# A hybrid decoder trunk on one core: where the norm's blocks turn between two layers, and in which order they come back

## The chip, the core and the metric

The kernel runs on one core of a Trainium2 chip. The metric is device time in microseconds; a run is one execution of the whole program. Five engines work side by side, each through its own list of instructions in order: TensorE (PE, with its weight loads as PEld), VectorE (DVE), ScalarE (ACT), GpSimd (POOL) and SyncE (SP). POOL and SP here mainly issue DMAs, each on a queue of its own: POOL's is the software queue q0, SP's the hardware queue q1.

## The reference

A trunk of two layers over 256 tokens of width 2048, in float32. Layer 0 mixes with gated linear attention, layer 1 with forgetting attention, whose keys and values come from the residual stream after layer 0. Every layer also attends to 256 memory tokens, and ends in a gated channel mixer. What stands around the change is this:

```python
def fox_shared_kv(x, g_kv, w_kv, b_f):
    hs = rmsnorm(x, g_kv)
    k, v, fl = split_cols(hs @ w_kv, [FOX_WIDTH, FOX_WIDTH, FOX_HEADS])
    ...

def rmsnorm(x, g):
    xf = x.astype(jnp.float32)
    y = xf * lax.rsqrt(jnp.mean(xf * xf, axis=-1, keepdims=True) + EPS)
    return (y * g.astype(jnp.float32)).astype(x.dtype)
```

`x` is the residual stream after layer 0's channel mixer, whose last step is a down-projection of hidden width 5632 to 2048, added to `x`. `FOX_WIDTH` is 1536: twelve heads of 128.

## The kernel before, in words

**Arithmetic.** Each float32 product is made of three TensorE products: data and weights are both split into a high and a low part, and high by high, high by low and low by high are added. Weights come from device memory in units of 512 KB (`split_unit`: load on SP's queue, L224, into one of four buffers `raw`; the high part is copied on ScalarE, L229; the low part subtracted on VectorE, L230). A unit's buffer is free for the next load once both are done. TensorE's matmuls of a panel of 512 output columns are at L333 (`panel_tm`): for 128 x 512 output there is a pair of token halves and a chain over chunks of 128 input features.

**The residual and its blocks.** `x[f]`, f = 0 to 3, holds 512 columns each, tokens on the partitions. The next layer needs features on the partitions. So each block f, once its two token halves are added (`add_to`, L483), goes through `then(f, b)` in `preparing`: the halves' squares are summed on ScalarE (`StreamNorm.add`, L608), each half is transposed in squares of 32 on VectorE (L1586) into a buffer `blk`, and, after the second half, `far_away` (L629 to L640) writes the block to device memory (L632) on POOL's queue. `land()` takes the oldest block that is away and issues its four returns (L637), which bring it back with the squares rearranged. `take()` takes the oldest block that landed and splits it, with the norm's gain, into four chunks of `hk`, whose buffers the profile calls B (ScalarE L524, VectorE L526). Block f gives chunks 4f to 4f+3. The buffer `blk` exists twice, so that block 2's transposes need block 0's way out to have landed, and block 3's need block 1's. Blocks 0 to 2 land in three parts of the tile `fvt`, block 3 in a tile called `fky`.

**The order at the seam.** The first layer's channel mixer, `ffn(0)`, ends with a pair of down panels (`down_pair`, blocks 0 and 1, evacuated through `late`) and two single ones, `f2` and `f3`, for blocks 2 and 3, each of six units. The hooks are written out by hand:

```python
for u in (4, 5):
    f2(u)
    then.land()
for u in range(2, 6):
    f3(u)
    if u % 2:
        then.take()
```

Then `fox` begins with its key panels, `two_tm([fk(0), fk(1)], 8, 2, hooks)`: two panels of eight units of two chunks each, interleaved, the second starting behind, with hooks at chosen units: the other returns and takes, and the row of the norm (`nx.row`, two matmuls at L593). A scheduler orders the built program by priorities and by what each step needs, so that the order in the source is a wish, and the built order can differ from it.

**The parked memory.** The first layer's hidden values need more chunks than there are buffers. So two tiles of projected memory, `mk1` and `mv1`, are stored to device memory before `ffn(0)`, their places carry four chunks more (`moremk`, `moremv` in the profile), and `fox` reloads them, 512 KB each, on POOL's queue (L1141 to L1143). They are needed only where layer 1 attends to the memory.

Of the kernel before, what the change touches and what calls it, by code (L numbers as in the profile page):

```python
# [20 lines left out]
P = 128  # L21
# [124 lines left out]
def _trunk(ctx: ExitStack, tc: tile.TileContext, xt, xtok, memt, wp, wgu, gns, gfin, cnv, par, msk, out):  # L146
# [984 lines left out]
    def fox(nx, vt, stash):  # L1131
        hk, hq, mix = bufB, bufA, bufB
        with (
# [4 lines left out]
            cdram = dp.tile([FOX_H, T], F32, name="cdram")  # L1138
            kt = fp.tile([P, FOX_H, T], F32, name="fkt")

            for t, tag, far in ((mk, "mk1", parked[0]), (mv, "mv1", parked[1])):  # L1141
                t[1] = const.tile(list(t[1].shape), F32, name=tag + "again", tag=tag)
                nc.gpsimd.dma_start(t[1].rearrange("p a b -> p (a b)"), far)  # L1143
            spare = [const.tile([P, 4, 4, 2, 32], F32, name="fky", tag=t) for t in ("mk0", "mv0")]
            last = blocks_of(kt[:, 8:].rearrange("p h t -> p (h t)"))
            open_ = []
# [1 line left out]
            def fk(j):  # L1148
                y, z = (spare[0], spare[1]) if j == 0 else (last, spare[0 if j == 1 else 1])

                return panel_tm(("fk", j), hk, turn_out(y, lambda back: open_.append((j, back, z))), j == 1)
# [9 lines left out]
            def query_input(i):  # L1161
                split_turned(hq, i, (*stash, spare[1])[i // 4], "mix1")

            two_tm([fk(0), fk(1)], 8, 2, {(0, 2): nx.land, (0, 3): nx.take, (1, 2): nx.row,
                                          (1, 3): lambda: nx.land(spare[1]), (1, 5): nx.take})
            step = fk(2)
            for u in range(8):
# [22 lines left out]
            for j, (lo, hi) in enumerate(FV_PARTS):  # L1190
                def fv_out(b, a, j=j, lo=lo, hi=hi):
                    S.activation(vt[:, b, lo:hi], a[:, : hi - lo], AF.Copy, scale=nx.col()[:, b : b + 1])
                    if j == 0:
                        take(b, a[:, hi - lo :])
                        if b:
                            forget()

                step = panel_tm(("fv", j), hk, fv_out)
                for u in range(8):
                    step(u)  # L1200
                    if (j, u) in ((0, 0), (0, 2), (1, 2)):
                        keys()
                    if j == 0:
                        query_input(4 + u)

# [106 lines left out]
    def down_pair(l, p, f, src, sums, flip, pool, temps, then=None):  # L1312

        def early(bank):
            t0, t1 = temps()
            S.activation(t0, bank["p1"], AF.Copy)
            add_to(f)(0, t0)
            V.tensor_tensor(t0, bank["p6"], t0, ALU.add)
            V.tensor_tensor(t1, bank["p7"], t0, ALU.add)
            add_to(f)(1, t1)  # L1320
            add_to(f + 1)(1, t1)
            add_to(f + 1)(1, bank["p5"])
            V.tensor_tensor(t0, bank["p5"], t0, ALU.add)
            add_to(f + 1)(0, t0)

        def late(b, h, a):
            add_to(f + h)(b, a)
            if then is not None:
                then(f + h, b)

        return pair_steps(where["down", l, p, f], src, sums, flip, pool, early, late)
# [26 lines left out]
    def ffn(l, nx, h, m, ys, zs, landing, then, pool, temps, last=None, spare=None):  # L1358
        with tc.tile_pool(name=f"ffn{l}", bufs=1) as fp:
# [159 lines left out]
            if l:  # L1519
                f2, f3 = [rows_tm(("down", l, p, f), src, evac) for f, evac in ((2, third), (3, last))]  # L1520
            else:
                f2 = panel_tm(("down", l, p, 2), src, third)
                f3 = panel_tm(("down", l, p, 3), src, lambda b, a: (add_to(3)(b, a), then(3, b)))
            for k in range(8):
# [14 lines left out]
            if l:  # L1539
                for u in (4, 5):  # L1540
                    f2(u)
                for b in range(2):
                    for u in range(2 if b else 4, 6):
                        f3(u, (b,))
            else:
                for u in (4, 5):
                    f2(u)
                    then.land()
                for u in range(2, 6):
                    f3(u)  # L1550
                    if u % 2:
                        then.take()

    def preparing(name, dst, pool, far, kept=None, tag="blk", queue=nc.sync):

        n = StreamNorm()  # L1560
        blocks = {}
        away, landed = [], []

        def land(z=None):

            f, back = away.pop(0)
            if z is None:
                z = pool.tile([P, 4, 4, 2, 32], F32, name="turn", tag="turn", bufs=2) if kept is None else kept[f]
            with tc.issue_after(loads[-1].ins) if queue is nc.sync else nullcontext():
                back(flat(z))  # L1570
            landed.append((f, z))

        def take():

            f, z = landed.pop(0)
            with tc.issue_after(casts[-1].ins):
                for k in range(4):
                    split_turned(dst, 4 * f + k, z, name)

        def then(f, b):  # L1580
            n.add(f, b)
            with tc.high_priority(offset=AHEAD):
                if b == 0:
                    blocks[f] = pool.tile([P, 4, 4, 2, 32], F32, name="blk", tag=tag, bufs=2)
                y = blocks[f]
                V.transpose(y[:, :, :, b, :], x[f][:, b, :].rearrange("p (k c i) -> p c k i", c=4, i=32))  # L1586
                if b:
                    away.append((f, far_away(far, flat(y), T, queue)))

        n.land = then.land = land  # L1590
        n.take = then.take = take
        return n, then
# [31 lines left out]
    with tc.tile_pool(name="store", bufs=1) as op:  # L1624
        gf = []
        free = list(range(8))

        def spare():
            return place("A", free.pop(0), "spare").rearrange("p a t -> p (a t)")

        def begin():
            for f in range(4):
                gf.append(place("A", 12 + f, "gf", F32).rearrange("p a t -> p (a t)"))
                nc.sync.dma_start(gf[f], gfin[:, f * 512 : (f + 1) * 512].to_broadcast([P, 512]))

        def temps(i):
            return op.tile([P, 512], F32, name="temp", tag=f"temp{i}")

        junk = op.tile([P, 1], F32, name="junk")

        def then(f, b):
            fin.add(f, b)
            if f == 0 and b == 0:
                S.activation(junk, fin.sums[:, 0, 0:1], AF.Sqrt)
            V.tensor_tensor(x[f][:, b, :], x[f][:, b, :], gf[f], ALU.mult)

        def last(b, a):

            part = sm.tile([P, 1], F32, name="fp", tag="fp")
            V.tensor_reduce(part, fin.sums[:, b, :6], axis=mybir.AxisListType.X, op=ALU.add)  # L1650
            V.tensor_scalar(part, part, 1.0 / D, EPS, ALU.mult, ALU.add)
            v = sm.tile([P, 2], F32, name="fv", tag="fv")
            for i in range(2):
                s = slice(i * T, (i + 1) * T)
                V.tensor_tensor(x[3][:, b, s], x[3][:, b, s], a[:, s], ALU.add)
                sq = sm.tile([P, T], F32, name="sq", tag="sq", bufs=2)
                S.activation(sq, x[3][:, b, s], AF.Square, accum_out=fin.sums[:, b, 6 + i : 7 + i])
            for i in range(2):
                V.scalar_tensor_tensor(v[:, i : i + 1], fin.sums[:, b, 6 + i : 7 + i], 1.0 / D,
                                       v[:, 0:1] if i else part, ALU.mult, ALU.add)  # L1660
            v = v[:, 1:2]
            r = sm.tile([P, 1], F32, name="root", tag="root")
            S.activation(r, v, AF.Sqrt)
            V.reciprocal(r, r)
            c = sm.tile([P, 1], F32, name="fc", tag="fc")
            V.scalar_tensor_tensor(c, v, r, r, ALU.mult, ALU.mult)
            V.tensor_scalar(c, c, -0.5, 1.5, ALU.mult, ALU.add)
            V.tensor_tensor(r, r, c, ALU.mult)
            for f, lo, hi in ((0, 0, T), (1, 0, 512), (0, T, 512), (2, 0, 512), (3, 0, 512)):
                t = x[f][:, b, lo:hi]  # L1670
                if f == 1:
                    S.activation(t, t, AF.Copy, scale=r)
                elif f < 3:
                    V.tensor_scalar(t, t, r, None, ALU.mult)
                else:
                    V.scalar_tensor_tensor(t, t, r, gf[3], ALU.mult, ALU.mult)
                (nc.scalar if f == 1 else nc.sync).dma_start(out[b, :, f * 512 + lo : f * 512 + hi], t)

        ys, zs = ([const.tile([P, 4, 4, 2, 32], F32, name="yzu", tag=f"{t}{i}") for i in range(2)] for t in ("mk", "mv"))
        then.begin = begin  # L1680
        more = [op.tile([P, 2, T], F32R, name=f"more{i}") for i in range(RING - KC)]
        ffn(1, n, bufA, bufB + more, ys, zs, zs, then, op, temps, last, spare)


# [69 lines left out]
```

## Time and profile before

| what | us |
|---|---|
| three runs | 2239.08, 2239.3, 2239.31 |
| median | 2239.3 |
| the profiled execution | 2237.85 |
| its span | 2236.1 |
| TensorE busy in it | 2212.4 |
| VectorE, ScalarE, POOL busy | 1781.5, 1419.7, 137.2 |

The span is that of the instructions; 1.75 us of the execution lie around it. Times within a view are microseconds from the start of the span. In a timeline's row stand start, length, engine, line, operation, tiles and count, and in brackets how long the engine was idle before and what released it. A row of the chain of waits says start, length and what; "issue" is time in which an engine waited for nothing that the profile shows.

### The profile page before, as it was taken

What the parts mean: (1) busy time and instruction counts of PE and PEld (TensorE: products, weight loads), DVE (VectorE), ACT (ScalarE), POOL (GpSimd) and SP (SyncE); (2) the same over time, 40 slices, a digit from 0 to 9 for tenths busy, and PEclk for the clock granted to TensorE, in tenths of its full rate; (3) what the DMA queues carried; (4) which work ended last, traced back from release to release, by engine and by line L of the source; (5) the groups of instructions that cost most, each with busy time, mean ns of one, the idle gap of its engine ahead of it and who ended that gap; (6) DMA issues with size and microseconds to landing.
All of it is one profiled execution on the core that took longest, in us unless ns stands there. A gap on an engine that the chain in (4) does not pass through costs nothing.

```text
span 2236.1 us, 30039 instructions
## 1 busy us (share of the span) xinstructions
PE 2212.4 (99%) x10323; PEld 1853.4 (83%) x10323; DVE 1781.5 (80%) x2638; ACT 1419.7 (63%) x2255; POOL 137.2 (6%) x259
## 2 busy tenths in 40 slices
PE   9999999999999999999999999999999999999998
PEld 7888888888788888888877998888878888888886
DVE  7768977688887889888868559668898788978876
ACT  6655664556786567665665455455787647676466
POOL 0000000001100001100111000000100000110010
PEclk9999999999999999999999999999999999999999
DMA  9867567777677567766677767777677756765674
GB/s 347 252 220 226 195 187 245 245 244 240 216 248 251 197 212 254 228 220 215 229 245 252 217 199 247 221 243 240 222 231 240 246 196 233 259 231 208 223 240 160
DMA packets 165633, 515.47 MB, mean 231 GB/s; under 512 B 20700, under 2 KB 41832, under 8 KB 165480
## 3 DMA queue, kind: packets, MB, share of 16 engines
q1 hardware_dynamic: 148200, 460.32, 62.1%
q0 software_dynamic: 16704, 52.44, 7.6%
q8 instruction: 81, 1.33, 0.2%
q10 hardware_dynamic: 576, 0.79, 0.1%
q14 instruction: 72, 0.59, 0.1%
HBM read 469.68 MB, written 43.79 MB: 230 GB/s over the span
## 4 chain that ended last, share of the span: by engine, by line
PE 91%; ACT 4%; issue 2%; DMA 2%; DVE 0%; POOL 0%; SPq 0%; ACTq 0%; DVEq 0%; POOLq 0%
PE acc L400 27%; PE acc L333 24%; PE ps_s L400 14%; PE ps_o L400 7%; PE ps_t L400 7%; PE acc L305 3%; PE acc L260 3%; PE ps_s L333 2%; ACT tap L1376 2%; PE acc L258 1%; DMA fvt<-far 1%; ACT whi L229 1%; PE acc L361 1%; DMA yzu<-far 1%; PE ps_s L1007 0%
## 5 line engine op out<-in xcount | busy, mean ns | idle before, releaser
L230 DVE TENSOR_TENSOR wlo<-raw,whi 128x1024 fp32r<-128x1024 f32 (+4 forms) x739 | 874.9, 1195 | 296.7 <-ACT whi L229 270.2
L229 ACT ACTIVATE whi<-raw 128x1024 fp32r<-128x1024 f32 (+4 forms) x739 | 761.4, 1037 | 448.2 <-PE acc L333 165.8
L333 PE MATMUL acc<-whi,B 128*128 128x512 f32 (+3 forms) x1248 | 294.9, 371 | 8.7 <-ACT B L524 8.7
L333 PEld LDWEIGHTS acc<-whi,B 128*128 128x128 f32 x1248 | 228.1, 189 | 37.5 <-ACT B L524 9.1
L375 ACT ACTIVATE whi<-raw 128x1024 fp32r<-128x1024 f32 (+1 forms) x136 | 129.8, 955 | 196.6 <-PE acc L400 78.3
L400 PE MATMUL acc<-whi,B 128*128 128x512 f32 x794 | 203.3, 390 | 1.4 <-ACT whi L229 1.3
L376 DVE TENSOR_TENSOR wlo<-raw,whi 128x1024 fp32r<-128x1024 f32 (+1 forms) x136 | 148.0, 1089 | 71.0 <-ACT whi L375 62.4
L400 PE MATMUL acc<-whi,mix 128*128 128x512 f32 x754 | 192.6, 390 | 0.9 <-ACT whi L229 0.7
L400 PEld LDWEIGHTS acc<-whi,B 128*128 128x128 f32 x794 | 148.5, 188 | 34.6 <-ACT whi L229 3.8
L400 PEld LDWEIGHTS acc<-whi,mix 128*128 128x128 f32 x754 | 141.3, 188 | 32.3 <-ACT whi L229 2.6
L333 PE MATMUL acc<-wlo,B 128*128 128x512 f32 (+3 forms) x624 | 159.8, 370 | 0.0
L1376 ACT ACTIVATE tap<-yzu,cw 128x256 f32<-128x256 f32 x264 | 124.5, 530 | 6.2 <-DMA yzu<-far 6.0
L1376 ACT ACTIVATE tap<-fvt,cw 128x256 f32<-128x256 f32 x264 | 124.4, 530 | 4.9 <-DMA fvt<-far 4.9
L333 PEld LDWEIGHTS acc<-wlo,B 128*128 128x128 f32 x624 | 114.9, 188 | 14.6
L1383 DVE TENSOR_TENSOR tap<-tap,tap 128x1024 f32<-128x1024 f32 x88 | 106.9, 1214 | 18.8 <-ACT tap L1376 18.8
L400 PE MATMUL acc<-wlo,B 128*128 128x512 f32 x397 | 112.3, 390 | 0.0
L400 PE MATMUL ps_s<-whi,mix 128*128 128x512 f32 x394 | 107.3, 389 | 0.0
L400 PE MATMUL acc<-wlo,mix 128*128 128x512 f32 x377 | 106.6, 390 | 0.0
L400 PE MATMUL ps_s<-whi,B 128*128 128x512 f32 x342 | 94.2, 389 | 0.0
L400 PEld LDWEIGHTS acc<-wlo,B 128*128 128x128 f32 x397 | 74.4, 188 | 15.9 <-DVE wlo L230 0.5
L400 PEld LDWEIGHTS ps_s<-whi,mix 128*128 128x128 f32 x394 | 74.0, 188 | 15.7
L400 PEld LDWEIGHTS acc<-wlo,mix 128*128 128x128 f32 x377 | 70.6, 188 | 15.2 <-DVE wlo L230 0.5
(490 smaller groups left out, 3756.0 us busy)
## 6 DMA issues: line engine op xcount, KB each, us to landing
raw<-wp SPq DMA_DIRECT2D x743, 512.0 KB, 4.5
fvt<-far POOLq DMA_DIRECT2D x100, 128.0 KB, 5.4
raw<-wp SPq DMA_DIRECT2D x32, 384.0 KB, 3.4
far<-yu POOLq DMA_DIRECT2D x22, 512.0 KB, 5.6
far<-yzu POOLq DMA_DIRECT2D x22, 512.0 KB, 5.8
yzu<-far POOLq DMA_DIRECT2D x88, 128.0 KB, 5.0
raw<-wp SPq DMA_DIRECT2D x24, 388.0 KB, 3.7
x<-xtok SPq DMA_DIRECT2D x8, 512.0 KB, 5.7
```

The lines of the kernel that those rows point to most:

```text
L229: casts.append(S.activation(hi[:, s], raw[:, s], AF.Copy))
L230: lows.append(V.tensor_tensor(lo[:, s], raw[:, s], hi[:, s].bitcast(F32), ALU.subtract))
L258: mm = TE.matmul(acc[p][c][:, :T], w[:, s], both[:, 0, :], start=False, stop=end and j == 3)
L260: mm = TE.matmul(acc[p][c], w[:, s], both, start=u == j == 0, stop=end and j == 3)
L305: mm = TE.matmul(acc[b][:, :n], src[kcs[j] - base][:, part, b * P : (b + 1) * P], w, start=u == 0 and low == part == j == 0, stop=u == end ...
L333: mm = TE.matmul(acc[b][:, :n], src[kc - base][:, part, b * P : (b + 1) * P], ready[low][:, j * n : (j + 1) * n], start=i == low == part = ...
L361: mm = TE.matmul(acc[b][:, :n], src[kc - base][:, part, b * P : (b + 1) * P], w, start=i == low == part == j == 0, stop=i == end and low = ...
L375: casts.append(S.activation(hi[:, :n], src, AF.Copy))
L376: lows.append(V.tensor_tensor(lo[:, :n], src, hi[:, :n].bitcast(F32), ALU.subtract))
L400: r = TE.matmul(bank[name], x, w, start=name not in begun, stop=last)
L1376: S.activation(by_run(taps[i][:, s, c, i:]), zs[slot][:, :, 2 * c + s], AF.Copy if i else AF.Identity, bias=0.0 if i else w[3], scale=w[2 ...
L1383: V.tensor_tensor(taps[0], taps[0], taps[n][:, :, :, :T], ALU.add)
```

## The change

1. The two reloads of parked memory are written behind unit 3 of the second value panel, not ahead of the key panels.
2. In `preparing`, a block may have a room of its own (`rooms`) in place of one of the two buffers `blk`. `ffn(0)` gives one each to blocks 2 and 3, in tiles called `tblk` whose places (`dsum4` and `dsum10`) the mixer's earlier sums leave free.
3. In `down_pair.late`, the add of the second panel's first token half (block 1) is held back behind block 0's last transpose.
4. The hooks: the third return of `ffn(0)` (block 2's) is issued ahead of unit 5 of `f3`, with the first take there; the two takes on odd units go, and `fox` takes at units 0 and 3 of its first panel and lands only block 3.

```diff
@@ fox
-            for t, tag, far in ((mk, "mk1", parked[0]), (mv, "mv1", parked[1])):
-                t[1] = const.tile(list(t[1].shape), F32, name=tag + "again", tag=tag)
-                nc.gpsimd.dma_start(t[1].rearrange("p a b -> p (a b)"), far)
...
-            two_tm([fk(0), fk(1)], 8, 2, {(0, 2): nx.land, (0, 3): nx.take, (1, 2): nx.row,
+            two_tm([fk(0), fk(1)], 8, 2, {(0, 0): nx.take, (0, 3): nx.take, (1, 2): nx.row,
                                           (1, 3): lambda: nx.land(spare[1]), (1, 5): nx.take})
...
                     if (j, u) in ((0, 0), (0, 2), (1, 2)):
                         keys()
+                    if (j, u) == (1, 3):
+                        for t, tag, far in ((mk, "mk1", parked[0]), (mv, "mv1", parked[1])):
+                            t[1] = const.tile(list(t[1].shape), F32, name=tag + "again", tag=tag)
+                            nc.gpsimd.dma_start(t[1].rearrange("p a b -> p (a b)"), far)
@@ down_pair
         def late(b, h, a):
-            add_to(f + h)(b, a)
+            held_back = then is not None and h and not b and then.rooms is not None
+            with tc.issue_after(then.turned[-1].ins) if held_back else nullcontext():
+                add_to(f + h)(b, a)
             if then is not None:
                 then(f + h, b)
@@ ffn
             else:
+                for f, k in zip((2, 3), SEVEN_DOWN):
+                    then.rooms[f] = lambda k=k: fp.tile([P, 4, 4, 2, 32], F32, name="tblk", tag=f"dsum{k}")
                 f2 = panel_tm(("down", l, p, 2), src, third)
...
                     f2(u)
                     then.land()
                 for u in range(2, 6):
+                    if u == 5:
+                        then.land()
+                        then.take()
                     f3(u)
-                    if u % 2:
-                        then.take()
@@ preparing
         n = StreamNorm()
-        blocks = {}
+        blocks, rooms, turned_blocks = {}, {}, []
...
                 if b == 0:
-                    blocks[f] = pool.tile([P, 4, 4, 2, 32], F32, name="blk", tag=tag, bufs=2)
+                    blocks[f] = rooms[f]() if f in rooms else pool.tile([P, 4, 4, 2, 32], F32, name="blk", tag=tag, bufs=2)
                 y = blocks[f]
-                V.transpose(y[:, :, :, b, :], x[f][:, b, :].rearrange("p (k c i) -> p c k i", c=4, i=32))
+                turned_blocks.append(V.transpose(y[:, :, :, b, :],
+                                                 x[f][:, b, :].rearrange("p (k c i) -> p c k i", c=4, i=32)))
                 if b:
                     away.append((f, far_away(far, flat(y), T, queue)))
...
+        n.rooms = then.rooms = rooms
+        then.turned = turned_blocks
```

For the second layer's channel mixer, `then.rooms` is set to none.

More of the change, by code (lines that the diff above doesn't have):

```diff
@@ L1679, in _trunk @@
         ys, zs = ([const.tile([P, 4, 4, 2, 32], F32, name="yzu", tag=f"{t}{i}") for i in range(2)] for t in ("mk", "mv"))
-        then.begin = begin
+        then.begin, then.rooms = begin, None
         more = [op.tile([P, 2, T], F32R, name=f"more{i}") for i in range(RING - KC)]
```

## The prediction

> **What bounds the kernel now.** I read the page's header and its table of groups first, to see which engine carries the time and where that engine waits.
>
> ```profile
> span 2236.1 us, 30039 instructions
> PE 2212.4 (99%) x10323; PEld 1853.4 (83%) x10323; DVE 1781.5 (80%) x2638; ACT 1419.7 (63%) x2255; POOL 137.2 (6%) x259
> L333 PE MATMUL acc<-whi,B 128*128 128x512 f32 (+3 forms) x1248 | 294.9, 371 | 8.7 <-ACT B L524 8.7
> ```
>
> TensorE is busy for 2212.4 of 2236.1 us, so little else can be won by moving things. Idle time in front of one group stands out: 8.7 us, ended by the scaled copy of a returned block (L524). It is one gap, at the seam between the first layer's last down panels and the second layer's keys, and every line of the diff acts at that seam. Next I read the chain of waits there (start, duration, what).
>
> ```profile
> 1159.21 0.56 POOL far L632
> 1159.76 5.12 issue
> 1164.90 0.54 POOL mk1again L1143
> 1165.46 0.53 POOL far L632
> 1166.00 1.65 POOL fvt L637 x3
> 1167.65 10.57 DMA fvt<-far
> 1178.32 0.52 ACT B L524
> 1178.88 8.18 PE acc L333 x26
> ```
>
> Block 0 goes out at 1159.21. On the same POOL queue follow the reload of the first parked tile, block 1's way out, then block 0's four returns. The last return takes 10.57 us and lands at 1167.65+10.57 = 1178.22; TensorE restarts 1178.88−1178.22 = 0.66 us later. Then TensorE's timeline, and the granted clock in windows cut where it changes (columns: window, length, PE, PEld, DVE, ACT, POOL busy, then granted clock, DMA share, GB/s).
>
> ```profile
> 1159.13 1.98 PE L333 MATMUL acc<-whi,moremk 128*128 128x512 f32 x8
> 1160.94 1.07 PE L333 MATMUL acc<-wlo,moremk 128*128 128x512 f32 x4
> 1161.85 1.98 PE L333 MATMUL acc<-whi,moremv 128*128 128x512 f32 x8
> ...
> 1169.56 0.61 PE L333 MATMUL acc<-wlo,mix 128*128 128x512 f32 x2
> 1178.88 3.36 PE L333 MATMUL acc<-whi,B 128*128 128x512 f32 x7 [8.71 <-ACT B L524]
> ...
> 1186.44 0.62 PE L333 MATMUL acc<-whi,B 128*128 128x512 f32 x2
> ```
>
> ```profile
> 1170.20:1172.90 2.70, 0.00 (x0) 0.00 (x0) 0.00 (x0) 1.41 (x5) 0.00 (x0) 1.00 1.04 367
> 1172.90:1178.80 5.90, 0.00 (x0) 0.00 (x0) 3.93 (x10) 1.39 (x6) 2.78 (x5) 0.50 1.02 328
> 1178.90:1183.10 4.20, 4.20 (x10) 3.33 (x11) 4.20 (x20) 2.72 (x7) 0.84 (x2) 0.50 1.04 331
> 1183.20:1186.40 3.20, 3.20 (x15) 2.63 (x15) 2.96 (x11) 2.52 (x5) 1.24 (x3) 1.00 0.95 300
> ```
>
> TensorE stops at 1169.56+0.61 = 1170.17 and waits 8.71 us. The granted clock falls to a half 2.7 us into the gap and is full again some 4.3 us after the restart. The first twelve matmuls shown took 1161.85−1159.13 = 2.72 us, 0.227 each. Block 0's twenty-four (chunks B0 to B3) ran from 1178.88 to 1186.44, 7.56 us, where 24 × 0.227 is 5.44: the slow clock costs 2.1 us. So the gap costs 8.7+2.1 = 10.8 us, all that this change can win. The other thing to see is the DMA share, 0.95 to 1.04 from 1170 to 1186: the sixteen DMA engines are full throughout, and 512 KB at 328 GB/s cost 1.6 us.
>
> The last views are POOL's timeline and the DMA issues (KB each, us from issue to landing), in order of issue: block 0 out, first parked reload, block 1 out, block 2 out, block 1's returns, block 3 out, block 2's returns.
>
> ```profile
> 1168.19 0.57 POOL L1143 DMA_DIRECT2D mv1again<-parkmv  x1
> 1168.75 0.55 POOL L632 DMA_DIRECT2D far<-blk  x1
> 1174.42 1.67 POOL L637 DMA_DIRECT2D fvt<-far  x3 [5.11 <-DMA far<-blk]
> 1176.74 0.55 POOL L637 DMA_DIRECT2D fvt<-far  x1 [0.65 <-DMA fvt<-far]
> 1177.99 0.56 POOL L632 DMA_DIRECT2D far<-blk  x1 [0.70 <-DVE nt L558]
> 1182.26 2.18 POOL L637 DMA_DIRECT2D fvt<-far  x4 [3.71 <-DMA far<-blk]
> 1186.49 2.17 POOL L637 DMA_DIRECT2D fky<-far  x4 [2.06 <-DMA far<-blk]
> ```
>
> ```profile
> far<-blk POOLq DMA_DIRECT2D x1, 512.0 KB, 3.2
> mk1again<-parkmk POOLq DMA_DIRECT2D x1, 512.0 KB, 6.3
> far<-blk POOLq DMA_DIRECT2D x1, 512.0 KB, 8.4
> far<-blk POOLq DMA_DIRECT2D x1, 512.0 KB, 13.2
> fvt<-far POOLq DMA_DIRECT2D x4, 128.0 KB, 8.8
> far<-blk POOLq DMA_DIRECT2D x1, 512.0 KB, 8.0
> fvt<-far POOLq DMA_DIRECT2D x4, 128.0 KB, 4.3
> ```
>
> The same 512 KB land after 3.2 us when the queue is empty and after 8.4 or 13.2 when it is not: the queue is served in order. Landings are 1164.90+6.3 = 1171.2 (reload), 1165.46+8.4 = 1173.9 (block 1 out), 1178.2 (block 0 back), 1168.75+13.2 = 1182.0 (block 2 out), 1176.74+8.8 = 1185.5 at the latest (block 1 back), 1177.99+8.0 = 1186.0 (block 3 out). Block 1 is back before TensorE needs it at 1186.44, so today there is one gap only.
>
> **The change part by part.** *The parked reloads.* In the source they move behind the value panels, but in the built program both stay on POOL near where they were: the first directly behind block 0's way out, the second behind block 1's. The scheduler lifts them to the first point their tiles allow. So this part moves 1 MB nowhere: nothing won or lost.
>
> *The order of the returns.* Built order on POOL before: block 0 out, reload, 1 out, 0 back, reload, 2 out, 1 back, 3 out, 2 back, 3 back. After: block 0 out, reload, **0 back**, 1 out, reload, 2 out, **3 out**, 1 back, 2 back, 3 back. Block 0's return has one 512 KB transfer fewer ahead, block 1's one more. The first is worth the slot of block 1's way out, 1173.9−1171.2 = 2.7 us: block 0 lands at 1178.2−2.7 = 1175.5, TensorE restarts at 1176.2 (idle 6.0 us). That idle is still longer than 2.7 us, so the clock is down and the 24 matmuls again take 7.56 us: B0 to B3 end at 1183.7.
>
> *The second return.* TensorE's built order has nothing else between B3 and B4 (after the change the second key panel and the norm's row matmuls come behind B11), so it waits for block 1. On POOL that return stands behind block 3's way out, which needs the last panel's transposes, and it cannot be read back until its own way out, and block 0's returns before it, have landed. By its landing seven 512 KB transfers of this queue have been served: two reloads, blocks 1, 2 and 3 out, 0 and 1 back. Before, the same seven were through at 1186.0, with the engines full. That is the price if nothing else competes; but weight loads will.
>
> *Rooms of their own for blocks 2 and 3, and the held-back add.*
>
> ```profile
> 1157.64 0.65 DVE L483 TENSOR_TENSOR x<-x,ps_t 128x512 f32<-128x512 f32 x1
> 1173.95 0.71 DVE L1586 STREAM_TRANSPOSE blk<-x 128x512 f32<-128x512 f32 x1 [4.18 <-DMA far<-blk]
> 1168.93 0.33 SPq L224 DMA_DIRECT2D raw<-wp  x1
> 1176.39 0.33 SPq L224 DMA_DIRECT2D raw<-wp  x1
> 1186.23 0.33 SPq L224 DMA_DIRECT2D raw<-wp  x1
> ```
>
> The add that now follows block 0's transposes takes 0.65 us; block 0 goes out up to that much earlier. But the reload behind it waits until its tile's last reader ends (1160.94+1.07 = 1162.01) and was issued only at 1164.90, so this earliness reaches nobody: cost and gain nought, at most 0.65 if the reload shifts too. Block 3's transposes no longer wait 4.18 us for block 1's way out. Queued on VectorE behind that wait is a weight split, and behind the split the next load's buffer: no load was issued between 1168.93 and 1176.39, nor between there and 1186.23. After the change the first of these comes 4.2 us earlier (1172.2) and the next by the 2.7 us of the earlier restart (1183.5). Both then share the full engines with the returns. One 512 KB load more before block 1 is back costs 1.6 us, two 3.2; none leaves 1186.0. I take two, because both times lie before 1186: block 1 lands at 1189.2, and B4 starts 0.66 later at 1189.9, against 1186.44: +3.4.
>
> *The second gap's clock.* From 1183.7 to 1189.9 TensorE idles 6.2 us, more than the 2.7 after which the clock fell, so the ramp is paid again: +2.1. If the clock stayed up this would be nought. [...]
>
> *The rest.* Squares and takes move among each other on ScalarE and VectorE without change in number; they lie beside a waiting TensorE: nought. Blocks 2 and 3 come right behind block 1, a slot of some 1.6 us apart (512 KB at 328 GB/s), while TensorE needs 5.4 us or more for each block: no third gap.
>
> Sum: +3.4+2.1 = +5.5 us. The profiled execution took 2237.85 us (span 2236.1 and 1.75 around it), 1.4 below the median of 2239.3; +5.5 gives 2243.4 for it and **2244.8** on the median. With one load instead of two it is +3.9, with four +8.7.
>
> **The rivals.** 0.2%, 4.5 us, is about what a measurement of this kernel can tell from no change.
>
> *Block 1 back in time (not slower).* If the queue's seven transfers are not the limit, block 1's return is issued when block 0 is back and block 1's way out has landed (1175.5+2.7 = 1178.2), takes the 4.3 us of block 2's returns, plus four issues of 0.55: 1184.7 at worst, B4 at 1185.4, −1.0, with too short a second gap (1.7 us) for the clock to fall. At best there is no second gap at all and the whole 2.7 of the earlier restart stays. It decides from a landing at 1185.8 (1186.44−0.66), and wholly at 1183.0. For it: block 2's 4.3 us. Against it: that row ran after the load traffic thinned, and the rows of the full stretch show 8.8. [...] Chance 0.17: −2.7 to −1.0.
>
> *Slow second return without the fall of the clock, or with one load only.* +3.4 to +3.9. Chance 0.10.
>
> *The whole row comes early (faster).* POOL's first reload was issued 1164.90−1162.01 = 2.9 us after its tile was free. If the new order lets it go at once, everything behind it moves up by 2.9 on top of the 2.7, block 1's return with it, so that no second gap opens: −5.6. It decides if the reload is issued by 1162.1. For it: nothing in the profile explains the 2.9. Against it: its place in POOL's and TensorE's order is unchanged, so whatever holds it stays. Chance 0.11.
>
> *The reloads really out of the way* would take most of the 10.8 us; the built order excludes it, and I give it no chance of its own.
>
> **How the numbers follow.** The forecast, slower by more than 4.5 us, has the remaining 0.62: +4.5 to +8.7, centre +5.5. Range: from −2.7 (2236.6) to +8.7 (2248.0); it leaves out the 0.11 below and less than 0.1 above. Slower cases alone: 2243.8 to 2248.0. Faster 0.11, same 0.17+0.10 = 0.27, slower 0.62.
>
> **What would show it.** In the changed profile: TensorE's first idle 6.0 instead of 8.7 us before B0; a new idle of about 6 us before B4, released by the same L524; granted clock 0.50 twice; block 3's way out ahead of block 1's returns, and two weight loads between 1171 and 1186. It is wrong if block 1's returns land within 7 us of TensorE's restart, if the second gap is under 2.7 us, or if the first reload is issued before 1163.

## The result and the profile after

The changed kernel takes 2243.46 us (median of 17 runs, 2242.11 to 2246.22); the kernel before, run beside it, 2239.3 (17 runs, 2237.51 to 2241.4). The ratio is 1.0019 with a 95% interval of 1.0011 to 1.0026: slower by 4.2 us, with 0.2% inside the interval. The profiled execution took 2243.66, near its median, and that of before lay 1.4 under its own, so the profiles differ by 5.8 us.

The page of the changed kernel, header and the group that held the one gap:

```profile
span 2241.9 us, 30033 instructions
PE 2216.0 (99%) x10323; PEld 1855.5 (83%) x10323; DVE 1781.2 (79%) x2638; ACT 1419.2 (63%) x2255; POOL 137.1 (6%) x259
L333 PE MATMUL acc<-whi,B 128*128 128x512 f32 (+3 forms) x1248 | 296.9, 373 | 10.9 <-ACT B L524 8.5
```

TensorE's busy time has grown by 3.6 us for the same 10323 matmuls, so the slow clock costs more; and the idle time before this group has grown from 8.7 to 10.9. TensorE's timeline shows where:

```profile
1169.46 1.07 PE L333 MATMUL acc<-wlo,mix 128*128 128x512 f32 x4
1177.93 3.35 PE L333 MATMUL acc<-whi,B 128*128 128x512 f32 x7 [7.40 <-ACT B L524]
...
1185.93 0.62 PE L333 MATMUL acc<-wlo,B 128*128 128x512 f32 x2
1187.64 0.73 PE L333 MATMUL acc<-whi,B 128*128 128x512 f32 x2 [1.08 <-ACT B L524]
1190.75 2.41 PE L333 MATMUL acc<-whi,B 128*128 128x512 f32 x5 [2.38 <-DVE B L526]
```

The first gap is 1.3 us shorter (7.40, it was 8.71). A second gap follows B3, in two pieces: 1.08 until ScalarE gives B4's high part, and 2.38, with two matmuls between, until VectorE gives its low part. The granted clock in windows cut where it changes:

```profile
1173.90:1177.90 4.00, 0.00 (x0) 0.00 (x0) 0.00 (x0) 0.53 (x2) 0.53 (x1) 0.50 1.01 381
1177.90:1184.00 6.10, 6.07 (x14) 4.79 (x15) 4.37 (x17) 4.94 (x14) 2.69 (x5) 0.50 1.02 387
1184.10:1187.60 3.50, 2.46 (x11) 1.67 (x9) 2.10 (x5) 1.47 (x3) 3.50 (x7) 1.00 0.83 214
1187.60:1190.80 3.20, 0.78 (x3) 0.35 (x3) 2.84 (x13) 3.20 (x9) 0.59 (x2) 1.00 1.01 279
1190.90:1194.20 3.30, 3.30 (x8) 2.60 (x9) 3.30 (x16) 2.67 (x7) 0.00 (x0) 0.50 0.66 175
```

After the first restart TensorE works 6.1 us at half clock (4.3 before, from 1178.88 to 1183.15), after the second another 3.3. B0 to B3 take 8.62 us from first start to last end (1177.93 to 1186.55) where they took 7.72 (1178.88 to 1186.60): +0.9. The account at the seam: −1.3 (first gap) +0.9 (first ramp) +3.5 (second gap) +1.7 (half of 3.3 us, the second ramp) = +4.8. The matmuls behind the seam start 5.5 us later than before, those ahead of it 0.35 later, so 5.1 came at the seam and 0.3 is not attributed. This is the account of one profiled execution; what kernels with the same order spread by is said below.

POOL's timeline and its DMA issues (the last figure is us to landing):

```profile
1165.25 0.57 POOL L1203 DMA_DIRECT2D mk1again<-parkmk  x1 [5.73 <-PE acc L333]
1165.88 2.21 POOL L637 DMA_DIRECT2D fvt<-far  x4
1168.08 0.56 POOL L632 DMA_DIRECT2D far<-blk  x1
1168.63 0.57 POOL L1203 DMA_DIRECT2D mv1again<-parkmv  x1
1169.19 0.53 POOL L632 DMA_DIRECT2D far<-tblk  x1
1174.36 0.53 POOL L632 DMA_DIRECT2D far<-tblk  x1 [4.64 <-DMA mk1again<-parkmk]
1180.24 2.21 POOL L637 DMA_DIRECT2D fvt<-far  x4 [5.35 <-DMA far<-blk]
```

```profile
mk1again<-parkmk POOLq DMA_DIRECT2D x1, 512.0 KB, 8.6
far<-blk POOLq DMA_DIRECT2D x1, 512.0 KB, 11.6
fvt<-far POOLq DMA_DIRECT2D x4, 128.0 KB, 4.7
```

Both reloads stayed on the way (`tblk` is a block's room of its own). The first lands after 8.6 us, not 6.3, with block 0's returns right behind it. Block 1's way out lands at 1168.08+11.6 = 1179.7 (before 1173.9), and only then can its returns be issued: 1180.24. They land at 1181.90+4.56 = 1186.46, just as B3 ends (1186.55).

### The profile page after: what moved, and what is told of

It is laid out like the page before. It is cut to its first block, busy times and chain, and to the rows that moved or that the text cites. A ratio compares the mean times of both kernels' runs of the same rounds, so it can differ in the third digit from the quotient of the medians.

```text
span 2241.9 us, 30033 instructions
## 1 busy us (share of the span) xinstructions
PE 2216.0 (99%) x10323; PEld 1855.5 (83%) x10323; DVE 1781.2 (79%) x2638; ACT 1419.2 (63%) x2255; POOL 137.1 (6%) x259
## 3 DMA queue, kind: packets, MB, share of 16 engines
q8 instruction: 81, 1.33, 0.2%
## 4 chain that ended last, share of the span: by engine, by line
PE 83%; issue 7%; ACT 4%; DMA 3%; DVE 1%; POOL 1%; ACTq 0%; DVEq 0%; POOLq 0%
PE acc L400 25%; PE acc L333 23%; PE ps_s L400 12%; PE ps_o L400 6%; PE ps_t L400 6%; PE acc L305 3%; PE acc L260 3%; PE ps_s L333 2%; ACT tap L1379 2%; PE acc L258 1%; ACT whi L229 1%; DMA raw<-wp 1%; DMA yzu<-far 1%; DMA far<-tblk 1%; DMA fvt<-far 1%
## 5 line engine op out<-in xcount | busy, mean ns | idle before, releaser
L230 DVE TENSOR_TENSOR wlo<-raw,whi 128x1024 fp32r<-128x1024 f32 (+4 forms) x739 | 875.6, 1196 | 305.0 <-ACT whi L229 287.8
L333 PE MATMUL acc<-whi,B 128*128 128x512 f32 (+3 forms) x1248 | 296.9, 373 | 10.9 <-ACT B L524 8.5
```

The lines of the kernel that those rows point to most:

```text
L230: lows.append(V.tensor_tensor(lo[:, s], raw[:, s], hi[:, s].bitcast(F32), ALU.subtract))
L333: mm = TE.matmul(acc[b][:, :n], src[kc - base][:, part, b * P : (b + 1) * P], ready[low][:, j * n : (j + 1) * n], start=i == low == part = ...
```

## The experiments

Each ran 11 times beside 33 runs of the kernel before on the same chip. Differences are of medians, in us.

| kernel | median | before | difference | ratio, 95% interval |
|---|---|---|---|---|
| changed (17 and 17 runs) | 2243.46 | 2239.3 | +4.2 | 1.0011 to 1.0026 |
| b_hold | 2239.08 | 2238.52 | +0.6 | 0.9995 to 1.0013 |
| b_rooms | 2236.93 | 2238.02 | −1.1 | 0.9988 to 1.0006 |
| a_newton | 2240.87 | 2238.52 | +2.4 | 1.0003 to 1.0021 |
| a_far3 | 2242.16 | 2238.52 | +3.6 | 1.0008 to 1.0026 |
| a_reload | 2238.42 | 2238.52 | −0.1 | 0.9988 to 1.0006 |
| a_reload_newton | 2236.84 | 2238.02 | −1.2 | 0.9986 to 1.0004 |
| a_reload_newton_pad | 2237.17 | 2238.02 | −0.9 | 0.9989 to 1.0006 |
| b_pad | 2238.11 | 2238.02 | +0.1 | 0.9992 to 1.0010 |
| b_warm | 2237.87 | 2237.91 | 0.0 | 0.9991 to 1.0008 |
| a_warm | 2241.34 | 2237.91 | +3.4 | 1.0003 to 1.0021 |
| b_rooms_warm | 2239.75 | 2237.91 | +1.8 | 1.0000 to 1.0017 |
| a_reload_newton_warm | 2236.97 | 2237.91 | −0.9 | 0.9988 to 1.0006 |

The profiled executions lie within 0.7 us of these medians, except a_newton (3.5 below its median), a_reload (2.2 below), and b_pad, a_reload_newton_pad and a_reload_newton_warm (1.4 to 1.6 below).

**Which parts act at all.** In the built programs, two of the four parts do nothing: with only the place of the reloads and the hooks changed, every engine's list of instructions is that of before; with everything but the hooks changed, every list is that of the changed kernel. What is left is the held-back add and the blocks' own rooms: four cells.

The held-back add alone (the reloads are written later as well, which changes no list):

```diff
+            held_back = then is not None and h and not b and then.rooms is not None
+            with tc.issue_after(then.turned[-1].ins) if held_back else nullcontext():
                 add_to(f + h)(b, a)
```

> The kernel before, with the held-back add alone (and the reloads written later, which the built order does not follow). The built order then already has block 0's returns ahead of block 1's way out, and block 1's returns ahead of block 3's way out. Theory G: the first gap is shortened as in the changed kernel (about 7.4 us), the second is small, so it is the gain of the change without most of its loss: 2237.5 to 2240. Rival L: the earlier weight loads that came with the blocks' own rooms are the cause of the loss, so without the rooms the whole earlier restart stays: 2236 to 2237.5. If the held-back add itself does the harm: 2243 and more.

The rooms alone (with the same place of the reloads):

```diff
+                for f, k in zip((2, 3), SEVEN_DOWN):
+                    then.rooms[f] = lambda k=k: fp.tile([P, 4, 4, 2, 32], F32, name="tblk", tag=f"dsum{k}")
```

> The kernel before, with rooms of their own for blocks 2 and 3 alone (built, it keeps the order of every engine; only block 3's transposes no longer wait for block 1's way out, 4.2 us in the profile of before, and the weight split behind them comes as much earlier). With the held-back add alone at 2239.1 against 2238.5 of before, and both at 2243.5, this completes the four cells. If the rooms themselves cost (one more weight load ahead of the returns takes 1.6 us of the full engines): 1 to 3 us above before, and the two parts add up. If they cost only together with the new order of the returns: within 1 us of before.

Neither alone can be told from no change (+0.6 and −1.1, both intervals hold 1); together they cost 4.2. They do not add up. It is the held-back add that puts block 0's returns ahead of block 1's way out; the rooms then let block 3's transposes run ahead of B0's low parts and block 3's way out ahead of block 1's returns. TensorE's waits with the add alone, and with the rooms alone:

```profile
1176.77 3.36 PE L333 MATMUL acc<-whi,B 128*128 128x512 f32 x7 [6.20 <-ACT B L524]
...
1186.14 0.73 PE L333 MATMUL acc<-whi,B 128*128 128x512 f32 x2 [1.09 <-ACT B L524]
1187.66 1.42 PE L333 MATMUL acc<-whi,B 128*128 128x512 f32 x5 [0.79 <-DVE B L526]
```

```profile
1176.89 3.35 PE L333 MATMUL acc<-whi,B 128*128 128x512 f32 x7 [7.76 <-ACT B L524]
```

With the add alone the second gap exists too, 1.9 us against the changed kernel's 3.5, and the clock stays up behind it (granted 1.00 from 1182.5 to 1198). With the rooms alone there is no second gap.

**VectorE's share of the second gap.** VectorE's timeline ahead of B4's low part, in the changed kernel and then with the held-back add alone:

```profile
1187.22 1.23 DVE L230 TENSOR_TENSOR wlo<-raw,whi 128x1024 fp32r<-128x1024 f32 x1 [1.32 <-ACT whi L229]
1188.36 0.15 DVE L558 TENSOR_TENSOR nt<-ny 128x2 f32<-128x2 f32 x1
...
1190.34 0.61 DVE L526 SCALAR_TENSOR_TENSOR B<-fvt,gains,B 128x128 fp32r<-128x128 f32 x2
```

```profile
1185.72 1.23 DVE L230 TENSOR_TENSOR wlo<-raw,whi 128x1024 fp32r<-128x1024 f32 x1 [0.41 <-ACT whi L229]
1186.87 0.15 DVE L561 TENSOR_TENSOR ny<-ny,nt 128x2 f32<-128x2 f32 x1
1187.05 0.16 DVE L558 TENSOR_TENSOR nt<-ny 128x2 f32<-128x2 f32 x1
1187.26 0.61 DVE L526 SCALAR_TENSOR_TENSOR B<-fvt,gains,B 128x128 fp32r<-128x128 f32 x2
```

Between the weight split and B4's low part stand ten steps of the norm's Newton chain in the changed kernel, 0.2 us each, from 1188.36 to the end of the last at 1190.13+0.16 = 1190.29; with the held-back add alone there are two. The next run queues the chain behind the take (`turned_lo` holds the low-part splits of the takes):

```diff
+            def norm_row():
+                with tc.issue_after(turned_lo[-1].ins):
+                    nx.row()
...
-            two_tm([fk(0), fk(1)], 8, 2, {(0, 0): nx.take, (0, 3): nx.take, (1, 2): nx.row,
+            two_tm([fk(0), fk(1)], 8, 2, {(0, 0): nx.take, (0, 3): nx.take, (1, 2): norm_row,
```

> The changed kernel, with VectorE's norm chain (sum, Newton steps, row) queued behind the low parts of block 1's take; nothing else is edited. Theory G (the loss is the second gap, made of a late block 1 and of ten steps of the norm chain ahead of B4's low part, plus a second ramp of the clock): B4's low part comes right behind the weight split, about 2 us earlier, the second gap falls from 3.5 to about 1.5 us, and the clock may stay up; 2.0 to 3.7 us less than the changed kernel's 2243.5, so 2239.8 to 2241.5. Rival L (the loss is in the transfers: the full DMA engines set when blocks 1 and 2 are back, and what VectorE does is covered): under 0.7 us less.

+2.4 instead of +4.2: 1.8 us less, just under the least that theory G gave (2.0), with overlapping intervals, so it is indicated and not proven. Its profile has the second gap in one piece of 1.89 us, but it is that of the shortest of its executions, 3.5 us under their median:

```profile
1176.19 3.35 PE L333 MATMUL acc<-whi,B 128*128 128x512 f32 x7 [5.90 <-ACT B L526]
1186.06 1.89 PE L333 MATMUL acc<-whi,B 128*128 128x512 f32 x7 [1.89 <-ACT B L526]
```

**Block 3's way out behind block 1's returns.** `backs` holds the return DMAs, `ends[f]` the last of block f.

```diff
+                    with tc.issue_after(ends[1].ins) if f == 3 and queue is nc.gpsimd else nullcontext():
                         away.append((f, far_away(far, flat(y), T, queue)))
```

> The changed kernel, with block 3's way out queued behind block 1's returns on POOL, as it was before the change. Theory G: block 1 lands a slot of 512 KB earlier, some 1.6 us, so by about 1184.9 on the profile's clock and in time for B4; the built VectorE order has only half of the norm chain ahead of B4's low part; the second gap falls below 1.5 us and the clock stays up: 3 to 5 us less than 2243.5, so 2238.5 to 2240.5. Rival N (the norm chain alone makes the gap): the chain still ends when it did, 2241 to 2243. Rival L: the returns' own time does not change and the weight loads take the slot, 2243.

+3.6, so the step on which I had put the price, one more transfer ahead of block 1, decides next to nothing. What holds block 1 is its own way out, which must land first (1179.7 in the changed kernel) and lands late. That block 0's returns and the reload ahead of it make it late is read from the order and not shown: in a_reload, below, with the reloads gone, it still took 9.5 us (1166.41 to 1175.9). Half the chain was gone here as well (second piece 1.23 us), and the first gap was 8.70, as long as before: the returns' landing spreads from kernel to kernel by more than the slot that was moved.

**The reloads really behind the returns.** `fky_back` is block 3's last return.

```diff
+                            with tc.issue_after(fky_back.ins):
                                 nc.gpsimd.dma_start(t[1].rearrange("p a b -> p (a b)"), far)
```

> The changed kernel, with the two reloads of parked memory queued on POOL behind block 3's returns, so that they really come back during the values. Two 512 KB transfers, and POOL's wait for the first reload's tile, no longer stand ahead of block 0's and block 1's returns. Theory G: block 0 can be issued as soon as its way out has landed (about 1162.5) and is back before TensorE has finished the last panel at 1170.5; both gaps shrink to what ScalarE and VectorE need, 1 to 3 us, with no fall of the clock: 6 to 9 us below the kernel before, 2230 to 2233. Rival L: weight loads fill the freed engines and the returns gain half: 2234 to 2238. Rival N: the norm chain stays in the way: 2236 to 2238.

−0.1: the whole loss is gone, with an interval (0.9988 to 1.0006) clear of the changed kernel's, but none of the 6 to 9 us below before was there. POOL and TensorE in it:

```profile
1157.88 0.56 POOL L634 DMA_DIRECT2D far<-blk  x1 [29.11 <-DVE blk L1596]
1164.23 2.19 POOL L639 DMA_DIRECT2D fvt<-far  x4 [5.79 <-ACT sq L608]
1166.41 0.56 POOL L634 DMA_DIRECT2D far<-blk  x1
```

```profile
1173.83 3.35 PE L333 MATMUL acc<-whi,B 128*128 128x512 f32 x7 [4.38 <-ACT B L524]
1183.27 2.83 PE L333 MATMUL acc<-whi,B 128*128 128x512 f32 x7 [2.20 <-ACT B L524]
```

These figures are from an execution 2.2 us under the median. Block 0's way out had landed at 1161.1, yet its returns were issued at 1164.23, so 3.1 us are lost, as some three are in every kernel here (the row names a square on ScalarE, but in the built program the returns wait for no square); the returns, without the reloads, still took 5.4 to 7.5 us beside the weight loads; and block 1, back at 1182.5, made a second gap of 2.20 and a second ramp. The wait moved from block 0 to block 1.

**With the chain moved too.** This is the two edits above together.

> The changed kernel, with both reloads queued behind block 3's returns and with the norm chain queued behind block 1's take: the two edits that gained, together. If the two losses are separate (5 us and 2.6 us below the changed kernel): 2235.5 to 2237. If the norm chain mattered only while block 1 came late (with the reloads away only two of its steps stand ahead of B4's low part): no better than the reloads alone, 2238.4.

−1.2 beside before; the interval holds 1. It is 5.3 us faster than the changed kernel by the medians' offsets, and no version here is shown to beat the kernel before. Beside the reloads alone (−0.1) the chain's place is not shown to matter here.

**What holds POOL for three microseconds.** Two runs add 24 small writes on POOL ahead of the first layer's mixer, to the kernel before and to the last kernel above.

```diff
+            pad = tp.tile([P, 4], F32, name="pad", tag="pad")
+            for _ in range(24):
+                nc.gpsimd.memset(pad, 0.0)
             for t, tag in ((mk, "mk1"), (mv, "mv1")):
```

> The kernel before, with 24 tiny memsets more on POOL, put ahead of the first layer's channel mixer, where POOL has time; nothing else is edited and the order of the DMAs is the same. It tests what holds POOL for some 3 us between block 0's way out and the next DMA, with all that it waits for done. In each profile so far one packet of 16 KB of an instruction queue starts as block 0's way out is issued. Theory F (POOL loads its next piece of code there): with the code moved by 24 instructions the load falls elsewhere, the first reload is issued at about 1162.4 instead of 1164.9, and block 0's return comes up to 2.6 us earlier: 1 to 3 us below before. Rival P (the hold belongs to the software DMA itself): still 2.9 us, no change.

> The same with the 24 memsets on POOL as well. Theory F: block 0's returns are issued when its way out has landed, about 1161.4 instead of 1164.2, and are back at about 1170, so TensorE's first idle falls from 4.4 to 1.5 us and the clock stays up there: 4 to 6 us below the kernel without them, 2231 to 2234. Rival P: no change. Rival L (the full engines set the landing): 1 to 2 us.

The gain that theory F gave came in neither. In the first, the reload came 5.7 us behind block 0's way out (1163.76−1158.06), as before (1164.89−1159.20); in the second, where no reload is in between, block 0's returns came 6.7 us behind it, and 7.0 without the writes.

```profile
1158.06 0.56 POOL L632 DMA_DIRECT2D far<-blk  x1 [28.93 <-DVE blk L1586]
1163.76 0.57 POOL L1143 DMA_DIRECT2D mk1again<-parkmk  x1 [5.14 <-PE acc L333]
```

What holds it stays open. The runs do not refute a load of POOL's code as such, for the packet that theory F goes by did not move: it starts 0.6 us ahead of block 0's way out before (1158.6) and 0.7 us ahead with the writes (1157.4). It may well be TensorE's, by my estimate from the page's counts: its queue (q8 on the page) carried 81 packets, 1.33 MB, in the whole run, and TensorE has 20646 matmuls and weight loads there, POOL 259 instructions.

**Keeping TensorE busy in the gap.** The same edit with N = 30 (in the kernel before), 26 (changed), 28 (rooms alone) and 16 (reloads and chain moved); the products are read by nobody.

```diff
+            idle = work("o")
+            with tc.issue_after(last_mm[-1].ins):
+                for i in range(N):
+                    TE.matmul(idle, bufB[KC - 1][:, 0, :P], bufB[KC - 1], start=i == 0, stop=i == N - 1)
```

What the profiles of before and of the changed kernel show for theory C, below (worked out from windows): their clock changed 3.41 us apart, or two or three times that (last section). In stretches of 3.41 us between these points, it fell at the end of stretches in which TensorE was busy for 20% (before), 4% and 25% (changed); it stayed down after 0% and 25% (before), 0% and 79% (changed), and rose after stretches that were busy throughout.

> The kernel before, with 30 matmuls that nobody reads between the last down panel's last matmul and B0's first, 30 x 0.227 = 6.8 us of the 8 us in which TensorE waits. It tests what the slow clock alone costs in the gap. Theory C (the clock falls after a window of some 3.4 us that is mostly idle, and is raised only after a window that is busy): it stays up, B0 to B3 take 5.4 us and not 7.6, and the gap's length stays: 2.1 us below before. Rival (block 1's return or VectorE is then late, since B4 is wanted 2 us earlier: block 1 was back at 1184.8 where B4 started at 1186.4): 1 us below before.

> The changed kernel, with 26 such matmuls (5.9 us of its 7.4) in the first gap. Theory C: the first ramp, 6.1 us at half clock, that is 3.0 us lost, goes, but B4's low part then is just as late as it was (VectorE's chain and block 1's landing do not move), so the second gap grows by nearly as much and the second ramp stays: 0 to 1 us below the changed kernel, still slower than before. Rival (the ramps are what makes the changed kernel slower, not the second gap): 3 to 4 us below the changed kernel, at the level of before.

> The kernel before with the rooms alone and 28 such matmuls in the gap. As for before: 2 us below the rooms alone, so 2235 to 2236 beside a before of 2238 to 2238.5; a half of it if block 1's return is late for the faster B0 to B3.

> The changed kernel with both reloads behind the returns, the norm chain behind block 1's take, and 16 such matmuls (3.6 us of a first gap of 5.4) on top. Theory C: half of the half-clock time of its profile (175.3 to 179.3 of the thousand, 3.9 us) is 2.0 us; block 1 lands at 1182.6 where B3 then ends at 1180.8, so most of it turns into a second gap: 0 to 1.5 us below the same kernel without them. Rival (B4 is not bound by block 1's landing): 2 us, 2235.

Before with 30 matmuls: no change, and the reason is not the one of either theory. The returns came at 1178.7, 2.15 us behind the extra matmuls, and the clock fell in that short gap all the same:

```profile
1170.22 6.96 PE L1147 MATMUL ps_o<-B 128*128 128x512 f32 x30
1179.32 3.36 PE L333 MATMUL acc<-whi,B 128*128 128x512 f32 x7 [2.15 <-ACT B L524]
```

```profile
1177.30:1179.00 1.70, 0.00 (x0) 0.00 (x0) 1.56 (x7) 0.33 (x3) 1.11 (x2) 1.00 1.04 422
1179.30:1182.60 3.30, 3.28 (x8) 2.56 (x9) 3.01 (x14) 2.76 (x7) 1.29 (x3) 0.51 1.03 288
```

The changed kernel with 26 went the same way (a gap of 3.04 us, the clock down from 1178.04) and stayed at +3.4. The rooms with 28 lost 2.9 us against the rooms alone (+1.8 and −1.1, with intervals that overlap): there the clock held at first, and the gain met later waits, 1.70 us for the norm's row matmuls and 0.55 for B4's low part, and then the clock fell after all, at 1187.80. In the fourth the clock never fell (granted 1.00 from 1166 to 1196), which makes it the clean test:

```profile
1169.10 3.79 PE L1148 MATMUL ps_o<-B 128*128 128x512 f32 x16
1173.99 2.00 PE L333 MATMUL acc<-whi,B 128*128 128x512 f32 x7 [1.11 <-ACT B L526]
1182.51 1.87 PE L333 MATMUL acc<-whi,B 128*128 128x512 f32 x7 [2.62 <-ACT B L526]
1189.58 1.87 PE L333 MATMUL acc<-whi,B 128*128 128x512 f32 x7 [1.34 <-ACT B L526]
```

Without these matmuls the clock was down from 1172.65 to 1179.48 in that kernel's profile, 4.2 us of it behind the restart at 1175.32. That ramp is gone and the time is the same (−0.9 against −1.2): waits of 2.62 us for block 1 and 1.34 for block 2 took its place, as theory C had it for the most part. In that kernel the next block's return sets the pace, not TensorE's clock.

## Why the prediction was right, and where its steps were off

The forecast was +5.5 (2244.8, range 2236.6 to 2248.0); measured are +4.2 and 2243.46. The interval of the ratio reaches from 0.11 to 0.26%, so it lies across the border that I had drawn between "slower" and "same" at 0.2%, and the median lies just under the +4.5 from which I had counted "slower". The shape was right: a shorter first gap, a new one before B4, a second fall of the clock. The reason that I gave for the new gap, and with it the size of that term, was mostly wrong, and the sum came near by luck. Of the terms:

- *The reloads stay.* Right, by the built lists and by POOL's timeline.
- *First gap, −2.7.* Mis-sized: −1.3. I gave the return the slot of block 1's way out, but took the first reload's own landing as fixed. It took 6.3, 5.8, 5.9, 7.2 and 5.3 us in the five kernels with block 1's way out behind it (before, b_rooms, b_pad, b_warm, b_rooms_warm) and 8.6, 9.4, 7.8, 7.5 and 9.2 in the five with the returns there (changed, a_far3, a_newton, b_hold, a_warm). So in these ten kernels the reload took longer where the returns follow it, 7.5 to 9.4 us against 5.3 to 7.2, which I read as transfers of this queue overlapping; one transfer's landing less another's is not a slot that can be taken out, and "the queue is served in order" does not give the landings. The −1.3 is itself one profile's figure: with the same POOL order ahead of block 0 the first gap was 8.70, 6.20 and 5.90 in a_far3, b_hold and a_newton, against 7.40 here.
- *B0 to B3 again 7.56.* Mis-sized by 0.9, since the ramp lasted 6.1 us; it was 5.7, 5.4 and 4.8 in a_far3, b_hold and a_newton. The clock rose 10.24 us after its fall in before and here alike, and here the restart came 4.13 us after the fall (1177.93−1173.80) where it came 5.97 after it in before (1178.88−1172.91).
- *Block 1 back at 1189.2, B4 waiting for it.* This step failed. Block 1 came 2.7 us earlier, at 1186.46, and its landing ended neither piece of the second gap. By the landing alone B4 would have started at 1186.46+0.66 = 1187.12, 0.57 behind B3's end (an estimate with the forecast's own 0.66); 3.46 us were measured and the forecast had 6.2. The first weight load came as forecast (1172.56 for 1172.2), the second only at 1185.37, not 1183.5, too late to matter. With one load the forecast's own sum is 1187.6. And by a_far3 the order against block 3's way out, on which I had built this step, was not its cause. (The norm's row matmuls stand inside B8 and not behind B11; nothing hangs on that.)
- *"The rest: nought."* This step failed. Squares and takes beside a waiting TensorE, I wrote; but B4's low part is VectorE's work, and the norm chain was put in front of it: the 2.38 us of the second piece. It made up for most of the 2.7 us by which block 1 came early. That two errors of opposite sign were nearly equal is luck.
- *The second ramp, +2.1.* It was 1.7, half of 3.3 us. I had taken over the ramp of before, which ran 4.27 us at half clock behind its restart (1178.88 to 1183.15).

A wait that I missed altogether is ScalarE's. Its timeline before, and then after:

```profile
1183.68 1.06 ACT L229 ACTIVATE whi<-raw 128x1024 fp32r<-128x1024 f32 x1 [2.05 <-PE acc L333]
1184.94 1.71 ACT L524 ACTIVATE B<-fvt,gains 128x256 fp32r<-128x256 f32 x4 [0.20 <-DMA fvt<-far]
```

```profile
1183.03 1.06 ACT L229 ACTIVATE whi<-raw 128x1024 fp32r<-128x1024 f32 x1 [1.16 <-PE acc L333]
1186.13 1.06 ACT L229 ACTIVATE whi<-raw 128x1024 fp32r<-128x1024 f32 x1 [2.05 <-PE acc L333]
1187.09 1.69 ACT L524 ACTIVATE B<-fvt,gains 128x256 fp32r<-128x256 f32 x4
```

Before, one weight copy stands between the restart and block 1's take; after, two, and the second waits until one of B3's last matmuls gives its buffer free. The take behind it cannot begin before 1187.09, so B4 is some 1 us late however early block 1 is back. The first piece of the second gap is 1.09 us as well in b_hold, a_far3 and a_reload_newton, where block 1 was back 0.4 to 0.8 us before B3's end and the same copy stands ahead of the take. No run took this copy away, so it is read from the traces and not tested.

Of the rivals, "block 1 back in time" did not come, but missed its border of 1185.8 by only 0.7 us; "the reloads really out of the way would take most of the 10.8 us" is refuted by a_reload; and the 2.9 us hold stayed, as the forecast had it. That the two parts cost only together is shown; how the 4.2 us divide among the late block 1, the norm chain and ScalarE's order is not settled, since single landings spread by 1 to 2 us between profiles (the reload's, with the returns behind it, from 7.5 to 9.4) and the chain's share has overlapping intervals.

## What to carry to other kernels

When a wait is shortened on a pipeline that is full, ask at once who is needed next, and on which engine each half of it is made: here the time won at block 0 was owed at block 1. Read the built order of every engine, not the queue alone, for what stands between a landing and the matmul that wants it. And moving an instruction in the source may move nothing in the program, while an innocent part (a held-back add) may reorder several engines.

## What the runs showed of the hardware

**In these profiles the clock changed at multiples of 3.41 us.** From before's fall at 1172.91 to its rise at 1183.15 are 10.24 us; in the changed kernel fall, rise, fall and rise lie at 1173.80, 1184.04, 1190.87 and 1194.28: steps of 10.24, 6.83 and 3.41, that is 3, 2 and 1 times 3.41. In nine other profiles, to about 0.03 us, the first rise came 10.24 us behind the first fall (a_far3), 6.83 (b_hold, a_newton, b_rooms, a_reload_newton, a_warm) or 3.41 (a_reload, b_warm, b_rooms_warm). The ramp behind the first gap cost 2.1 us in before and 3.0 in the changed kernel because the rise came 10.24 us behind the fall in both, and the restart 5.97 us behind it in the one and 4.13 in the other.

**The clock also fell after stretches in which TensorE was partly busy.** Each profile is cut here into stretches of 3.41 us, counted from a change of its clock, and TensorE's busy time is added in each (worked out from the timelines). The clock fell at the end of stretches that were 25% busy (changed kernel, second fall) and 43% busy (before with 30 extra matmuls, only 2.0 us after its last), and stayed up over one of 60% (held-back add alone). Between these the busy share alone did not sort them: the clock fell after 53% (a_far3, where a pair of matmuls took 0.61 us at 1185.61 and 1.05 at 1190.69) and stayed up over 51% (a_newton). It did not rise after a stretch of 79% (changed kernel, first restart) and rose after one of 96% (a_reload). So the clock was lost in a gap of 2.15 us in before with 30 extra matmuls, and in the changed kernel the restart, which left 21% of its stretch idle, had to wait for the end of the next one.
